# One transpose at a time between single products: a change to the order of TensorE's work in a hybrid encoder layer

## The chip, the cores and the metric

The kernel runs on one core of one Trainium2 chip. The metric is the device time of one execution in microseconds (us). The kernel before took 697.28 us, the median of three runs (695.9 to 697.84).

Names of engines are those of the profile: PE is the matrix engine (TensorE), PEld its loading of stationary operands, DVE, ACT and POOL the vector, scalar and GpSimd engines, SP the engine that issues most transfers. A "product" below is one matmul instruction of a projection.

## The reference

One layer over 512 tokens with 1024 features, in fp32. A pre-norm, one input projection whose columns belong to three groups of attention heads (A: differential, 4 heads; B: forgetting, 6 heads; C: chunked, 6 heads), one output projection into the residual, and then a gated MLP with a causal convolution and a gated per-layer input.

```python
hn = rms_norm(h, ln_mix)
z = hn @ w_in                     # 1024 x 3590
(q1, q2, k1, k2, va, qf, kf, vf, fg, qc, kc, vc) = jnp.split(z, IN_SPLITS, axis=-1)
# every q and k: rms_norm per head of 64
o_a = diff_attention(q1, q2, k1, k2, va, lam, subln_g, lam_init)
log_f = jax.nn.log_sigmoid(fg + fgate_bias)
o_b = forgetting_attention(qf, kf, vf, log_f)     # bias: cumulative sum of log_f
o_c = chunk_attention(qc, kc, vc, rel_bias)
h = h + jnp.concatenate([o_a, o_b, o_c], axis=-1) @ w_out
h = h + conv_gated_mlp(rms_norm(h, ln_ffn), w_up, conv_w, conv_b, w_down)
gate = jax.nn.sigmoid(rms_norm(h, ln_ple) @ w_ple_gate)
h = h + (p @ w_ple_proj) * gate
```

## The kernel before

An fp32 operand is split into a high and a low part, and each fp32 product is made of three products of those parts (`mm3`: high by high, high by low, low by high). The change touches only the first part of the kernel, in which the input projection, the attention and most of the output projection (six of eight blocks of its contraction) share PE.

**Slots.** The work that fills PE comes in slots. Slots 4 to 7 project the part A0b for the four blocks of 128 tokens (262 columns), 8 to 11 A1 (384 columns), 12 to 15 A1b (256), 16 to 27 B0, B1 and B2 and 28 to 39 C0, C1 and C2 (384 each), and slots 40 to 47 are units of the output projection (512 columns, `out_unit`). A projecting slot has eight steps j = 0 to 7 of three products; a slot of the output projection has six steps of three.

**Units between the steps.** The attention of a pair of heads is cut into generators. `qk_cols` brings q and then k into feature-major order: four transposes of 128x128 blocks of `zn` into one bank of PSUM (tile `..._q_p`, then `..._k_p`), then copies by ACT and DVE, then three moves of 64 rows by POOL. `forget_cumsum` transposes the log gates (`pf`), scans along the tokens on DVE (`fs`) and transposes back (`pq`). `scores` makes, for each block of queries, two matmuls into a bank with tag `s` (two buffers), and a softmax on DVE, ACT and POOL, whose result `e` POOL or DVE scales. `prob_cols` transposes the probabilities in three groups (`pt0`: 4 transposes, `pt1`: 3, `ptc`: 3), each followed by a copy on ACT (`pth`) and a subtraction on DVE (`ptl`). `values` multiplies them with V, in two steps of four matmuls. All transposes go into banks with tag `t` (three buffers).

**The order.** The table `T` gives each unit a slot and a step: `"B1a": (24, 1)` is the `qk_cols` of pair B1, from step 1 of slot 24. `run` (line 731) goes through the eight steps of a slot: it takes one step of the filling products, and then one step of the unit at the head of the slot's list, if its time has come. So a group of three or four transposes, with all that follows it up to the unit's next `yield`, stands behind three products. What the list holds after the eighth step is run to its end before the next slot begins, with no product between. PE's instructions are pinned in this order; those of ACT, DVE and POOL in this part are put in order by the framework.

**The rest of the kernel** (MLP, gate) follows with an order of its own by a planner's costs; the change leaves it as it is.

Of the kernel before, what the change touches and what calls it, by code (L numbers as in the profile page):

```python
# [15 lines left out]
P = 128  # L16
D = 1024
S = 512
NT = S // P
KD = D // P  # L20
# [12 lines left out]
C_MIX, C_QK, C_SUB, C_CONV0, C_CONV1, C_CONV2, C_PLE, C_CONVB, C_FFN, C_FGB, C_LAM, NSMALL = (  # L33
    0, 8, 14, 16, 60, 104, 148, 156, 200, 208, 214, 470)
# [43 lines left out]
def kernel(ctx: ExitStack, tc: tile.TileContext, x, xt0, xt, pt_in, small, bias_c,  # L78
# [33 lines left out]
    pe, act, dve, pool, sp = (Engine(e) for e in (nc.tensor, nc.scalar, nc.vector, nc.gpsimd, nc.sync))  # L112
# [30 lines left out]
    def col(c0, i=0):  # L143
        return cols[:, c0 + i : c0 + i + 1]
# [88 lines left out]
    def load_rect(w, k0, nk, c0, ncol, name, eng=dve, gain=None):  # L233
        rows = w[k0 * P : (k0 + nk) * P, c0 : c0 + ncol].rearrange("(k p) c -> p k c", p=P)
        return load_w(lambda raw: [(raw[:, : nk * ncol].rearrange("p (k c) -> p k c", k=nk), rows)],
                      nk, ncol, ncol, name, eng, gain)

    def mm3(acc, ah, al, bh, bl, first, last, **k):
        pe.matmul(acc, ah, bh, start=first, stop=False, **k)
        pe.matmul(acc, ah, bl, start=False, stop=False, **k)  # L240
        pe.matmul(acc, al, bh, start=False, stop=last, **k)
# [11 lines left out]
    def tcol(T, k, t):  # L253
        return T[k // 4][:, k % 4, t * P : (t + 1) * P]
# [164 lines left out]
    def feature_cols(zn, j, name):  # L419
        pt = bank("t", f"{name}_p")  # L420
        for t in range(NT):
            pe.transpose(pt[:, t * P : (t + 1) * P], zn[:, t, j * P : (j + 1) * P], ident)
        return pt

    def move(dst, src):
# [1 line left out]

    def split_q(zn, g, name):

        pt = feature_cols(zn, 0, name)  # L430
        q0, q1 = (ap.tile([P, S], F32R, tag="q", bufs=4, name=f"{name}_q{i}") for i in range(2))
        lo = ap.tile([P, S], F32R, tag="ql", bufs=1, name=f"{name}_ql")
        act.activation(q0, pt, AF.Identity, scale=g)
        dve.scalar_tensor_tensor(lo, pt, g, f32(q0), ALU.mult, ALU.subtract)
        move(q1[DN], q0[DN])
        move(q0[DN], lo[UP])
        move(q1[UP], lo[DN])
        return q0, q1

    def split_k(zn, g, name):  # L440

        pt = feature_cols(zn, 1, name)
# [14 lines left out]
    def project(ws, n, t, z, evac, prefetch):  # L457
        for k in range(KD):
            wh, wl = ws[k // 2]
            mm3(z[:, :n], tcol(Th, k, t), tcol(Tl, k, t), wh[:, k % 2, :], wl[:, k % 2, :], k == 0, k == KD - 1)  # L460
            if k < KD - 1:
                yield
        evac()
        for w in prefetch:
            w()
        yield
# [36 lines left out]
    def qk_cols(pr, part):  # L503
        need(*(("in", pr, part, t) for t in range(NT)))
        g = GAIN[pr[0]]
        zn = ZN[pr, part]
        q = split_q(zn, gq[:, g : g + 1], f"{pr}_q{part}")
        yield
        QK[pr, part] = (q, *split_k(zn, col(C_QK, g + 1), f"{pr}_k{part}"))
        yield  # L510


# [3 lines left out]
    def forget_cumsum():  # L516
        need(*(("in", "A0", 1, t) for t in range(NT)))
        xv = fg[:, :, 0:6]
        fa = ap.tile([P, NT, 6], F32, tag="fa", name="fa")
        dve.scalar_tensor_tensor(fa, xv, -1.0, xv, ALU.mult, ALU.max)  # L520
        act.activation(fa, fa, AF.Exp, scale=-1.0)
        act.activation(fa, fa, AF.Ln, bias=onec)
        dve.scalar_tensor_tensor(xv, xv, 0.0, fa, ALU.min, ALU.subtract)
        yield
        pf = bank("t", "pf")
        for t in range(NT):
            pe.transpose(pf[:, t * P : (t + 1) * P], fg[:, t, :], ident)
        fs = ap.tile([P, S], F32, tag="bias", bufs=3, name="fs")
# [6 lines left out]
        yield  # L535
        pq = bank("t", "pq")
        for t in range(NT):
            pe.transpose(pq[:, t * P : (t + 1) * P], fs[:, t * P : (t + 1) * P], ident)
        dve.tensor_copy(fq[:, :, 0:6], pq.rearrange("p (t c) -> p t c", t=NT)[:, :, 0:6])
        done("fc")  # L540
        yield
# [74 lines left out]
    def prob_cols(pr, hh):  # L616
        probs = PROB[pr, hh]
        tiles = []
        for kb in range(2):
            n = (NT - kb) * P  # L620
            pt = bank("t", f"{pr}_{hh}_pt{kb}")
            for qb in range(kb, NT):
                pe.transpose(pt[:, (qb - kb) * P : (qb - kb + 1) * P], probs[qb][:, kb * P : (kb + 1) * P], ident)
            th = ap.tile([P, S], F32R, tag="pth", bufs=3, name=f"{pr}_{hh}_pth{kb}")
# [4 lines left out]
            yield  # L629
        assert not PTC_OF  # L630
        PTC_OF.append((pr, hh))
        pt = bank("t", f"{pr}_{hh}_ptc")
        pe.transpose(pt[:, P : 2 * P], probs[3][:, 3 * P : 4 * P], ident)
        pe.transpose(pt[:, 2 * P : 3 * P], probs[2][:, 2 * P : 3 * P], ident)
        pe.transpose(pt[:, 3 * P : 4 * P], probs[3][:, 2 * P : 3 * P], ident)
# [67 lines left out]
    def out_unit(j, ks, wts, prefetch):  # L703

        acc = bank("zs"[j % 2] if ks[0] else "z", f"wo_{ks[0]}_{j}")
        c = slice(j % 4 * P, (j % 4 + 1) * P)
        for k in ks:
            wh, wl = (w[:, 0, c] for w in wts[k])
            mm3(acc, wh, wl, Th[k // 4][:, k % 4, :], Tl[k // 4][:, k % 4, :], k == ks[0], k == ks[-1])
# [14 lines left out]
    def step(early, g):  # L724
        if early:
            with tc.high_priority(offset=early):
                next(g)
        else:
            next(g)

    def run(fill, todo):

        todo = [(start, early, gen(*args)) for start, early, gen, args in todo]
        for j in range(8):
            next(fill, None)
            while todo and j >= todo[0][0]:
                try:
                    step(*todo[0][1:])
                    break
                except StopIteration:  # L740
                    todo.pop(0)
# [9 lines left out]
    T = {  # L751
# [139 lines left out]
    for n in range(2):  # L891
        for t in range(NT):
            wts = {k: wo[k, n] for k in range(6)}
            pre = []
            if n == 0:
                pre = [wo_load(k, 1) for k in ((0, 1), (2, 3), (4,), (5,))[t]]
            else:
                pre = [wo_load(6 + t // 2, t % 2)]
            if slot == T["C1v1"][0] + 1:
                split_o(6, 7, slice(0, S))  # L900
            run(out_unit(4 * n + t, range(6), wts, pre), steps.get(slot, []))
            slot += 1
            next_job()
    assert max(COPIES) < slot
# [923 lines left out]
```

## Time and profile before

| | |
|---|---|
| median of three runs | 697.28 us (695.9 to 697.84) |
| profiled execution, first to last instruction (span) | 692.9 us |
| PE busy | 678.8 us, 98% of the span |
| DVE, ACT, POOL busy | 560.7, 411.0, 238.7 us |
| granted TensorE clock | 1.000 |

No time beside its span is given for the profiled execution; the median of the runs is 4.4 us above the span. A row of the timeline or of a group of matmuls gives the start of the first one, the time until the end of the last one, and the number in it. Matmuls are pipelined and their ends are modelled, so costs on PE are read below from start to start. A wait stands in square brackets at the end of a row, with the instruction that ended it. In the tile names the numbers of pairs and heads are left out: `B_pt<-ident,B_e` is a transpose of probabilities of any B pair, `B_z` a projection.

### The profile page before, as it was taken

What the parts mean: (1) busy time and instruction counts of PE and PEld (TensorE: products, weight loads), DVE (VectorE), ACT (ScalarE), POOL (GpSimd) and SP (SyncE); (2) the same over time, 40 slices, a digit from 0 to 9 for tenths busy, and PEclk for the clock granted to TensorE, in tenths of its full rate; (3) what the DMA queues carried; (4) which work ended last, traced back from release to release, by engine and by line L of the source; (5) the groups of instructions that cost most, each with busy time, mean ns of one, the idle gap of its engine ahead of it and who ended that gap; (6) DMA issues with size and microseconds to landing.
All of it is one profiled execution on the core that took longest, in us unless ns stands there. A gap on an engine that the chain in (4) does not pass through costs nothing.

```text
span 692.9 us, 12202 instructions
## 1 busy us (share of the span) xinstructions
PE 678.8 (98%) x4244; PEld 617.7 (89%) x4244; DVE 560.7 (81%) x1168; ACT 411.0 (59%) x799; POOL 238.7 (34%) x349
## 2 busy tenths in 40 slices
PE   9999999999999999999999999999999999999997
PEld 8988989988999988878899899989998898999886
DVE  7678787888778875599788987898888889888863
ACT  7646766757656754475476655456664566556821
POOL 6586766757575540231211212211111210000210
PEclk9999999999999999999999999999999999999999
DMA  9554579746745174379999799998999884463441
GB/s 329 209 155 110 164 229 273 226 155 164 285 137 179 40 270 138 91 181 253 170 263 223 150 254 248 268 227 189 229 308 246 186 226 140 139 232 100 159 122 61
DMA packets 57112, 133.84 MB, mean 193 GB/s; under 512 B 6454, under 2 KB 8118, under 8 KB 57052
## 3 DMA queue, kind: packets, MB, share of 16 engines
q1 hardware_dynamic: 45660, 107.60, 47.3%
q0 software_dynamic: 11104, 25.17, 22.2%
q8 instruction: 33, 0.54, 0.3%
q10 hardware_dynamic: 288, 0.30, 0.1%
q14 instruction: 27, 0.22, 0.1%
HBM read 125.83 MB, written 44.05 MB: 245 GB/s over the span
## 4 chain that ended last, share of the span: by engine, by line
PE 83%; DVE 6%; POOL 3%; DMA 3%; ACT 2%; issue 2%; SPq 0%; POOLq 0%; DVEq 0%; ACTq 0%
PE u L104 22%; PE dn_X L104 9%; PE pg L104 6%; PE wo L104 6%; PE C_z L104 5%; PE sX L104 5%; PE dn_Y L104 4%; PE B_z L104 4%; PE sY L104 3%; PE sZ L104 3%; PE A_z L104 3%; PE dn_Z L104 2%; PE pp L104 2%; PE C_s L104 1%; DMA bias_B<-fk_d 1%
## 5 line engine op out<-in xcount | busy, mean ns | idle before, releaser
L104 DVE TENSOR_TENSOR w_lo<-w_raw,w_hi 128x768 fp32r<-128x768 f32 (+5 forms) x154 | 115.0, 786 | 9.4 <-ACT w_hi L104 9.2
L104 ACT CAST w_hi<-w_raw 128x768 fp32r<-128x768 f32 (+5 forms) x154 | 99.7, 687 | 33.8 <-PE dn_X L104 8.0
L104 PE MATMUL u<-Th,w_hi 128*128 128x512 f32 x224 | 87.0, 391 | 0.0
L104 PE MATMUL u<-Tl,w_hi 128*128 128x512 f32 x224 | 86.9, 390 | 0.0
L104 PE MATMUL u<-Th,w_lo 128*128 128x512 f32 x224 | 86.8, 390 | 0.0
L104 PEld LDWEIGHTS u<-Th,w_lo 128*128 128x128 f32 x224 | 42.0, 188 | 8.9
L104 PEld LDWEIGHTS u<-Th,w_hi 128*128 128x128 f32 x224 | 42.0, 188 | 8.6 <-ACT Th L104 0.4
L104 PEld LDWEIGHTS u<-Tl,w_hi 128*128 128x128 f32 x224 | 42.0, 188 | 8.1
L104 DVE SCALAR_TENSOR_TENSOR c<-u,cols,c 128x511 f32<-128x511 f32 (+1 forms) x56 | 41.0, 745 | 6.2 <-ACT c L104 5.7
L104 POOL DMA_DIRECT2D usum<-usum x16 | 13.0, 813 | 91.2 <-DMA usum<-in_w_up_dram 49.3
L104 PE MATMUL dn_X<-g_ah,w_hi 128*128 128x256 f32 x144 | 39.8, 276 | 0.0
L104 PE MATMUL dn_X<-g_ah,w_lo 128*128 128x256 f32 x144 | 39.8, 276 | 0.0
L104 PE MATMUL dn_X<-g_al,w_hi 128*128 128x256 f32 x144 | 39.8, 276 | 0.0
L104 PE MATMUL B_z<-B_h,Th 128*128 128x384 f32 x96 | 34.4, 358 | 0.7 <-DVE B_zn L104 0.6
L104 PE MATMUL C_z<-C_h,Th 128*128 128x384 f32 x96 | 34.3, 357 | 0.0
L104 PE MATMUL B_z<-B_h,Tl 128*128 128x384 f32 x96 | 32.3, 337 | 0.0
L104 PE MATMUL C_z<-C_h,Tl 128*128 128x384 f32 x96 | 32.3, 337 | 0.0
L104 PE MATMUL C_z<-C_l,Th 128*128 128x384 f32 x96 | 32.2, 336 | 0.0
L104 PE MATMUL B_z<-B_l,Th 128*128 128x384 f32 x96 | 32.2, 335 | 0.0
L104 POOL DMA_DIRECT2D dsum<-dsum x16 | 13.0, 814 | 53.5 <-DMA dsum<-dsum 24.5
L104 POOL TENSOR_TENSOR sums<-sums,n_sq 128x512 f32<-128x512 f32 x3 | 3.9, 1297 | 79.7 <-ACT n_sq L104 79.6
L104 ACT ACTIVATE c<-u,cols 128x512 f32<-128x512 f32 x28 | 21.5, 775 | 16.0 <-PE u L104 14.6
(504 smaller groups left out, 2385.4 us busy)
## 6 DMA issues: line engine op xcount, KB each, us to landing
w_raw<-in_w_up_dram SPq DMA_DIRECT2D x44, 384.0 KB, 6.9
dsum<-in_w_dsum_dram SPq DMA_DIRECT2D x12, 768.0 KB, 8.1
w_raw<-dsum SPq DMA_DIRECT2D x24, 384.0 KB, 5.9
usum<-in_w_usum_dram SPq DMA_DIRECT2D x32, 256.0 KB, 6.1
w_raw<-in_w_down_dram SPq DMA_DIRECT2D x18, 384.0 KB, 5.3
w_raw<-usum SPq DMA_DIRECT2D x16, 384.0 KB, 7.4
B_r<-in_w_in_dram SPq DMA_DIRECT2D x12, 384.0 KB, 3.7
C_r<-in_w_in_dram SPq DMA_DIRECT2D x12, 384.0 KB, 5.9
```

What stands on the lines that cost most here:

```text
L104: ins = getattr(self.eng, op)(*a, **k)
```

## The change

- `project` and `out_unit` yield after every product, not after every three (`mm3_singly`; a value `ONE` says that a group of three isn't finished).
- Every generator with transposes yields `ONE` after each transpose but the last of a group. The last one is emitted together with the copies that follow it, as before.
- Before the first transpose of a group stands a yield `NEXT_COLS`, or the unit starts in that state (`FIRST_AT`).
- `run` puts at most one transpose behind each product. A group in progress goes on behind every product; a new one begins behind the second product of a step, or behind the third, where all other units go on as before.
- What the list holds at the end of a slot is run on until a unit stands at a transpose (`ONE` or `NEXT_COLS`); it and all behind it are carried into the next slot, ahead of its own list, with step 0. Only the last slot runs all to the end.

The table `T`, the number of instructions and their operands stay as they are.

```diff
+    ONE, NEXT_COLS = "one", "cols"
+
+    def mm3_singly(acc, ah, al, bh, bl, first, last):
+        for i, (a, b) in enumerate(((ah, bh), (ah, bl), (al, bh))):
+            pe.matmul(acc, a, b, start=first and i == 0, stop=last and i == 2)
+            if i < 2:
+                yield ONE
...
         for t in range(NT):
             pe.transpose(pt[:, t * P : (t + 1) * P], zn[:, t, j * P : (j + 1) * P], ident)
+            if t < NT - 1:
+                yield ONE
         return pt
...
-            mm3(z[:, :n], tcol(Th, k, t), tcol(Tl, k, t), wh[:, k % 2, :], wl[:, k % 2, :], k == 0, k == KD - 1)
+            yield from mm3_singly(z[:, :n], tcol(Th, k, t), tcol(Tl, k, t), wh[:, k % 2, :], wl[:, k % 2, :], k == 0, k == KD - 1)
...
-        q = split_q(zn, gq[:, g : g + 1], f"{pr}_q{part}")
-        yield
-        QK[pr, part] = (q, *split_k(zn, col(C_QK, g + 1), f"{pr}_k{part}"))
+        q = yield from split_q(zn, gq[:, g : g + 1], f"{pr}_q{part}")
+        yield NEXT_COLS
+        k = yield from split_k(zn, col(C_QK, g + 1), f"{pr}_k{part}")
+        QK[pr, part] = (q, *k)
         yield
...
             for qb in range(kb, NT):
                 pe.transpose(pt[:, (qb - kb) * P : (qb - kb + 1) * P], probs[qb][:, kb * P : (kb + 1) * P], ident)
+                if qb < NT - 1:
+                    yield ONE
...
-        else:
-            next(g)
-
-    def run(fill, todo):
-
-        todo = [(start, early, gen(*args)) for start, early, gen, args in todo]
+                return next(g)
+        return next(g)
+
+    FIRST_AT = {qk_cols: NEXT_COLS, prob_cols: NEXT_COLS}
+    LEAD = 2
+
+    class Unit:
+
+        def __init__(self, start, early, gen, args):
+            self.start, self.early, self.g, self.at = start, early, gen(*args), FIRST_AT.get(gen)
+
+        def go(self):
+            try:
+                self.at = step(self.early, self.g)
+            except StopIteration:
+                self.at = "end"
+            return self.at
+
+    CARRY = []
+
+    def run(fill, todo, last=False):
+
+        todo = CARRY + [Unit(*q) for q in todo]
+        CARRY.clear()
         for j in range(8):
-            next(fill, None)
-            while todo and j >= todo[0][0]:
-                try:
-                    step(*todo[0][1:])
+            busy = False
+            for i in range(3):
+                more = next(fill, None)
+                if todo and (todo[0].at == ONE or todo[0].at == NEXT_COLS and j >= todo[0].start and not busy and i >= 3 - LEAD and more == ONE):
+                    busy = todo[0].at != ONE or busy
+                    todo[0].go()
+                if more != ONE:
                     break
-                except StopIteration:
-                    todo.pop(0)
+            while not busy and todo and todo[0].at != ONE and j >= todo[0].start:
+                if todo[0].go() != "end":
+                    break
+                todo.pop(0)
         for _ in fill:
             pass
-        for _, early, g in todo:
-            try:
-                while True:
-                    step(early, g)
-            except StopIteration:
-                pass
+        for i, q in enumerate(todo):
+            while q.at != "end":
+                if q.at in (ONE, NEXT_COLS) and not last:
+                    CARRY.extend(todo[i:])
+                    for q in CARRY:
+                        q.start = 0
+                    return
+                q.go()
```

More of the change, by code (lines that the diff above doesn't have):

```diff
@@ L428, in split_q @@
     def split_q(zn, g, name):
-        pt = feature_cols(zn, 0, name)
+        pt = yield from feature_cols(zn, 0, name)
         q0, q1 = (ap.tile([P, S], F32R, tag="q", bufs=4, name=f"{name}_q{i}") for i in range(2))
@@ L440, in split_k @@
     def split_k(zn, g, name):
-        pt = feature_cols(zn, 1, name)
+        pt = yield from feature_cols(zn, 1, name)
         k0, k1 = (ap.tile([P, S], F32R, tag="k", bufs=4, name=f"{name}_k{i}") for i in range(2))
@@ L523, in forget_cumsum @@
         dve.scalar_tensor_tensor(xv, xv, 0.0, fa, ALU.min, ALU.subtract)
-        yield
+        yield NEXT_COLS
         pf = bank("t", "pf")
@@ L527, in forget_cumsum @@
             pe.transpose(pf[:, t * P : (t + 1) * P], fg[:, t, :], ident)
+            if t < NT - 1:
+                yield ONE
         fs = ap.tile([P, S], F32, tag="bias", bufs=3, name="fs")
@@ L534, in forget_cumsum @@
         nc.sync.dma_start(out=fk_d, in_=nf)
-        yield
+        yield NEXT_COLS
         pq = bank("t", "pq")
@@ L538, in forget_cumsum @@
             pe.transpose(pq[:, t * P : (t + 1) * P], fs[:, t * P : (t + 1) * P], ident)
+            if t < NT - 1:
+                yield ONE
         dve.tensor_copy(fq[:, :, 0:6], pq.rearrange("p (t c) -> p t c", t=NT)[:, :, 0:6])
@@ L623, in prob_cols @@
                 pe.transpose(pt[:, (qb - kb) * P : (qb - kb + 1) * P], probs[qb][:, kb * P : (kb + 1) * P], ident)
+                if qb < NT - 1:
+                    yield ONE
             th = ap.tile([P, S], F32R, tag="pth", bufs=3, name=f"{pr}_{hh}_pth{kb}")
@@ L628, in prob_cols @@
             tiles.append((th[:, :n], tl[:, :n]))
-            yield
+            yield NEXT_COLS
         assert not PTC_OF
@@ L632, in prob_cols @@
         pt = bank("t", f"{pr}_{hh}_ptc")
-        pe.transpose(pt[:, P : 2 * P], probs[3][:, 3 * P : 4 * P], ident)
-        pe.transpose(pt[:, 2 * P : 3 * P], probs[2][:, 2 * P : 3 * P], ident)
-        pe.transpose(pt[:, 3 * P : 4 * P], probs[3][:, 2 * P : 3 * P], ident)
+        for c, qb, kb in ((1, 3, 3), (2, 2, 2), (3, 3, 2)):
+            pe.transpose(pt[:, c * P : (c + 1) * P], probs[qb][:, kb * P : (kb + 1) * P], ident)
+            if c < 3:
+                yield ONE
         th, tl = ptc
@@ L708, in out_unit @@
             wh, wl = (w[:, 0, c] for w in wts[k])
-            mm3(acc, wh, wl, Th[k // 4][:, k % 4, :], Tl[k // 4][:, k % 4, :], k == ks[0], k == ks[-1])
+            yield from mm3_singly(acc, wh, wl, Th[k // 4][:, k % 4, :], Tl[k // 4][:, k % 4, :], k == ks[0], k == ks[-1])
             if k != ks[-1]:
@@ L726, in step @@
             with tc.high_priority(offset=early):
-                next(g)
-        else:
-            next(g)
-    def run(fill, todo):
-        todo = [(start, early, gen(*args)) for start, early, gen, args in todo]
-        for j in range(8):
-            next(fill, None)
-            while todo and j >= todo[0][0]:
-                try:
-                    step(*todo[0][1:])
+                return next(g)
[15 more added lines that the diff above has]
+        CARRY.clear()
+        for j in range(8):
+            busy = False
[5 more added lines that the diff above has]
+                if more != ONE:
                     break
-                except StopIteration:
-                    todo.pop(0)
+            while not busy and todo and todo[0].at != ONE and j >= todo[0].start:
+                if todo[0].go() != "end":
+                    break
+                todo.pop(0)
         for _ in fill:
             pass
-        for _, early, g in todo:
-            try:
-                while True:
-                    step(early, g)
-            except StopIteration:
-                pass
+        for i, q in enumerate(todo):
[6 more added lines that the diff above has]
+                q.go()
     T = {
@@ L900 @@
                 split_o(6, 7, slice(0, S))
-            run(out_unit(4 * n + t, range(6), wts, pre), steps.get(slot, []))
+            run(out_unit(4 * n + t, range(6), wts, pre), steps.get(slot, []), n == 1 and t == NT - 1)
             slot += 1
```

## The prediction, made before the changed kernel was run

> **What bounds the kernel now.** I read the page first, then busy time by stretches, then PE's timeline around each wait in the part that changes.
>
> ```profile
> span 692.9 us, 12202 instructions
> ...
> PE 678.8 (98%) x4244; PEld 617.7 (89%) x4244; DVE 560.7 (81%) x1168; ACT 411.0 (59%) x799; POOL 238.7 (34%) x349
> ```
> ```profile
> 28.00:262.00 234.00, 225.32 (x1382) 208.85 (x1382) 188.76 (x575) 154.02 (x370) 150.57 (x223) 1.00 0.58 178
> 262.00:272.00 10.00, 10.00 (x52) 8.37 (x52) 7.53 (x14) 6.18 (x12) 0.21 (x1) 1.00 0.59 187
> 272.00:693.00 421.00, 416.47 (x2649) 375.19 (x2648) 346.25 (x541) 231.71 (x382) 69.81 (x82) 1.00 0.76 193
> ```
>
> PE is the bound: 98% busy at the full clock (1.00 behind the counts in the rows by stretches). The change acts from about 28 us (slot 6) to a little behind 262 us. Up to 262 us PE is idle for 234.00 - 225.32 = 8.7 us, behind it for 4.5 in 431; read from start to start the waits cost more, since a matmul that waited also has to load its operand afterwards. The change adds no instruction. It can win through the price of a transpose on PE, or through waits; it loses through prices and waits too. I take these in turn.
>
> **The price of a transpose.** Slot 40, with no wait in it:
>
> ```profile
> 243.87 0.60 PE L104 MATMUL C_pt<-ident,C_e 128*128 128x128 f32 x4
> 244.22 0.48 PE L104 MATMUL wo<-Th,wo_h 128*128 128x512 f32 x1
> 244.54 0.39 PE L104 MATMUL wo<-Tl,wo_h 128*128 128x512 f32 x1
> 244.77 0.39 PE L104 MATMUL wo<-Th,wo_l 128*128 128x512 f32 x1
> 245.00 0.49 PE L104 MATMUL C_pt<-ident,C_e 128*128 128x128 f32 x3
> 245.24 0.48 PE L104 MATMUL wo<-Th,wo_h 128*128 128x512 f32 x1
> 245.56 0.39 PE L104 MATMUL wo<-Tl,wo_h 128*128 128x512 f32 x1
> ```
>
> A product of 512 columns takes 244.77 - 244.54 = 0.23. From the first of four transposes to the second product behind them it is 0.67, so four cost 0.67 - 0.23 = 0.44; three cost 245.56 - 245.00 - 0.23 = 0.33. That is 0.11 each, with nothing left over for the change from transposes to products, within the rounding of the rows. The product behind a group starts early on paper (244.22) and takes 0.32 to the next one: it still sits out the last transpose. So the last transpose of a group, which already has a product behind it, costs as much as one with another transpose behind it, and I expect a single one to cost 0.11. By the diff and the loops there are 248 transposes, and the places where one is followed by something else go from 59 (one for each uninterrupted run) to 236. For the 177 new ones I take 0.005 us each, between 0 and the 0.01 that the rows can hide: **+0.9** (0 to +1.8). Less than nothing would need the cheaper transpose that is the first rival.
>
> By the Trainium skill, page "TensorE: Matmul & The Clock Gate", section "LDWEIGHTS (loading the stationary operand)", loading 128 columns takes 128/1.2 = 107 ns (an estimate from its formula). The spacing of 0.11 agrees with that; by that rule the product behind a single transpose has its own 107 ns of load uncovered, which speaks against any gain from singles.
>
> **Waits that should go.** Slot 20 ends with four scores of A1 run back to back:
>
> ```profile
> 109.67 0.28 PE L104 MATMUL A_0b_s<-A_k_k,A_q_q 128*128 128x256 f32 x1
> 109.79 0.28 PE L104 MATMUL A_0b_s<-kl,A_q_q 128*128 128x256 f32 x1
> 110.38 0.38 PE L104 MATMUL A_s<-A_k_k,A_q_q 128*128 128x256 f32 x1 [0.31 <-DVE A_st L104]
> 110.59 0.28 PE L104 MATMUL A_s<-kl,A_q_q 128*128 128x256 f32 x1
> 110.92 0.38 PE L104 MATMUL A_1b_s<-A_k_k,A_q_q 128*128 128x256 f32 x1
> ```
>
> A matmul of 256 columns takes 0.12. So 0.59 - 0.12 = 0.47 is lost for the bank, 0.21 - 0.12 = 0.09 for the late load, 0.33 - 0.12 = 0.21 for the next bank, and 0.1 for its load: 0.87. Now `prob_cols` of A1 is in mid-group at the end of slot 20 and is carried, with these scores behind it; they then stand between the steps of slot 21. I take **-0.8** (-0.9 to -0.5).
>
> Slots 24 and 25:
>
> ```profile
> 141.47 0.33 PE L104 MATMUL B_z<-B_h,Tl 128*128 128x384 f32 x1
> 141.64 0.40 PE L104 MATMUL B_po<-B_pth,B_V 128*128 128x512 f32 x1
> 142.30 0.50 PE L104 MATMUL B_po<-B_ptl,B_V 128*128 128x512 f32 x1 [0.26 <-DVE B_ptl L104]
> ...
> 144.38 0.34 PE L104 MATMUL B_z<-B_h,Tl 128*128 128x384 f32 x1
> 145.27 0.38 PE L104 MATMUL B_s<-B_k_k,B_q_q 128*128 128x256 f32 x1 [0.55 <-POOL B_k_k L104]
> ...
> 147.96 0.47 PE L104 MATMUL B_s<-B_k_k,B_q_q 128*128 128x512 f32 x1 [0.55 <-DVE B_st L104]
> ```
> ```profile
> 143.20 0.64 POOL L561 TENSOR_SCALAR_AFFINE_SELECT dg<-bias_B 128x512 f32<-128x512 f32 x1 [1.18 <-DMA bias_B<-fk_d]
> ```
>
> A product of 384 columns takes 0.17 (141.47 to 141.64). B1's q and k are now transposed in a heap at the end of slot 24. POOL's last move of k stands behind the mask `dg`, which waits for the transfer of its bias until 143.20, and the first scores of B1 wait 145.27 - 144.38 - 0.17 = 0.72, and 0.1 for the load. After the change B1's transposes are carried into the first three steps of slot 25, and all of its scores slide to that slot's end, well behind the moves: **-0.8** (-0.9 to 0). The price is that they stand there in a heap of four, where now only the last one does, with 0.55 idle. The nearest heap of four is that of slot 20, 0.87, with smaller blocks; DVE reads a B bank in two instructions, so I take 1.3 for the heap against the 0.7 (idle and load) now: **+0.6** (+0.2 to +0.9). The values of B0 lose 142.30 - 141.64 - 0.23 = 0.43 and the load for `ptl`, behind the DVE work of the heap of slot 24. That work is spread then, but the gap before them shrinks (below): **-0.3** (-0.5 to +0.5).
>
> The transposes of q that wait for their fourth block of `zn`:
>
> ```profile
> 166.93 0.49 PE L104 MATMUL B_q_p<-ident,B_zn 128*128 128x128 f32 x3
> 167.84 0.33 PE L104 MATMUL B_q_p<-ident,B_zn 128*128 128x128 f32 x1 [0.42 <-DVE B_zn L104]
> ```
> ```profile
> PE C_q_p L104 <- DVE C_zn L104: 0.7, 1, 0.7
> ```
>
> B2 loses 167.84 - 166.93 - 3 x 0.11 = 0.58, and C0, by 0.7 idle, more. In both, three products now stand between the first transpose and the fourth: 3 x 0.17 = 0.5 of work in the wait, **-1.0** for both (-1.2 to -0.5). A0b waits in the same way, but there the gain is given back:
>
> ```profile
> 43.91 0.33 PE L104 MATMUL A_q_p<-ident,A0b_zn 128*128 128x128 f32 x1 [0.66 <-DVE A0b_zn L104]
> ```
> ```profile
> 47.45 2.00 POOL L104 TENSOR_SCALAR A_k_k<-A_k_k 64x512 fp32r<-64x512 f32 x3
> ```
> ```profile
> 49.51 0.39 PE L104 MATMUL A_0b_s<-A_k_k,A_q_q 128*128 128x256 f32 x1
> ```
>
> `zn` sets 43.91; from there POOL's moves, in their order, run until 47.45 + 2.00 = 49.45, and the first scores with A0b start at 49.51. Whatever PE wins at 43.91 it waits at 49.51: **0**.
>
> **Waits that should grow.** A group now ends two to five products later against its neighbours, its copies start later, and whoever reads them stands where it stood. The scan of the forget gates:
>
> ```profile
> 59.93 0.66 PE L104 MATMUL pq<-ident,fs 128*128 128x128 f32 x4 [0.93 <-DVE fs L104]
> ```
> ```profile
> 58.66 1.21 DVE L104 TENSOR_TENSOR_SCAN fs<-f_ones,pf 128x512 f32<-128x512 f32 x1
> ```
>
> `pf` ends two products later (0.35), and `pq` still starts behind the last product of slot 11: **+0.3** (0 to +1.0, if DVE puts one of its 0.9 us splits ahead of the scan). Values that follow their transposes in the same slot, as for B1:
>
> ```profile
> 173.22 0.39 PE L104 MATMUL B_po<-B_ptl,B_V 128*128 128x512 f32 x1
> ```
> ```profile
> 172.26 1.15 DVE L104 TENSOR_TENSOR B_ptl<-B_pt,B_pth 128x512 fp32r<-128x512 f32 x2
> ```
>
> The first of these two subtractions, about 0.65 of the 1.15, ends near 172.9: 0.3 to spare, and the gap shrinks by two products, 0.35. So a wait of 0.05 and a load: **+0.2** (0 to +0.5); A0, with narrower products (0.12): **+0.1** (0 to +0.3). Scores behind the moves of k: A1b **+0.1** (0 to +0.5), and C2, where the transposes of q and k run over into slot 41:
>
> ```profile
> 251.74 0.39 PE L104 MATMUL wo<-Th,wo_l 128*128 128x512 f32 x1
> 252.55 0.39 PE L104 MATMUL C_s<-C_k_k,C_q_q 128*128 128x256 f32 x1 [0.41 <-POOL C_k_k L104]
> ```
> ```profile
> 251.88 0.61 POOL L104 TENSOR_SCALAR C_k_k<-C_k_k 64x512 fp32r<-64x512 f32 x1
> ```
>
> Here q ends one product later (0.23) and k five (1.15). POOL's last move ends at 252.49, after an unbroken row of six that q starts, so I take **+0.2** (0 to +1.1). The transposes of A1's q may find their bank still being read: **+0.1** (0 to +0.3).
>
> Sum: +0.9 - 0.8 - 0.8 + 0.6 - 0.3 - 1.0 + 0.3 + 0.2 + 0.1 + 0.1 + 0.2 + 0.1 = **-0.4 us**. Behind 262 us PE hardly ever waits, so a shift passes to the end: span 692.5. The profiled execution's span lies 4.4 us under the median of the runs, 697.28; so I forecast **696.9 us**, which is no change: 0.3%, about what a measurement of this kernel can tell from none, is 2.1 us. Adding the lower ends gives -3.3, the upper ones +5.9.
>
> **The rivals.**
>
> *The load is hidden.* If 0.11 is a load that a product in front can cover, only the transpose's own streaming is left. 512 columns take 0.23 and 256 take 0.12, so 128 stream in 0.055; 248 x 0.055 = 13.6 us less, 683.6. Against it stands that the first transpose of a group has a product in front and the group still costs 0.11 for each. The same page of the Trainium skill, in "Part 2: What happens when you issue a matmul", has PE pull loads ahead of running matmuls; by that rule a single transpose would be covered. The early start on paper of the product at 244.22 would fit it, the 0.32 behind it doesn't.
>
> *Waits go, and none comes.* Copies have slack, and PE gains 0.9 + 0.9 + 1.2 + 0.5, less 0.4 for the heap: -3.1, or 694.2. For it: DVE and ACT get their work in smaller lots. Against it: three of the slacks above are under 0.35.
>
> *The copies come late* (slower). The place: `pq`, the values of A0, B0 and B1, the scores of A1b and C2. It decides where the slack is under the delay of 0.35 (five products at C2). Priced at 1.0 for `pq`, 0.45 (0.35 and a load) for each of three values, 1.3 for the scores, 0.3 for the bank and 1.8 for the change-overs, 5.8, less the 2.0 that slots 20, 25, 28 and 32 still win net: +3.8, or 701.1. For it: A0b's k move and C2's end within 0.06 of the scores that need them. Against it: most groups feed values a slot later.
>
> **Numbers.** No change (696.9, alone 695.2 to 699.4): 0.41. Hidden load: 0.07. Waits go: 0.27. Copies late: 0.25. So faster 0.34, same 0.41, slower 0.25; the range from 693.0 to 701.5 takes in the other two rivals, leaves out the hidden load, and is a little narrower than all ends added, which won't fall together. The order that the framework gives DVE, ACT and POOL may move by more than these terms; that is why it isn't narrower.
>
> **What would show it.** A single transpose: from its start to the second product behind it one product and 0.11 (0.055 for the first rival). The waits for `A_st` near 110 and `B_k_k` near 145 are gone, and four scores of B1 stand in a row near 147 with two waits. The waits for `B_zn` near 168 and for `C_zn` are 0.5 shorter, that for `fs` near 60 is 0.3 longer. I am wrong if a transpose's price moves, or if DVE or POOL takes its work in another order, so that waits show at tiles that I don't name.

## The result, and the profile after

The changed kernel took **704.21 us** (median of four runs, 702.91 to 704.73); the kernel before, beside it, took 697.21. The ratio is **1.0107, 95% interval 1.0088 to 1.0125**: slower by 7.0 us, where no change was forecast. The time lies outside the range of 693.0 to 701.5.

The head of the page after:

```profile
span 703.0 us, 12202 instructions
```

The two spans differ by 703.0 - 692.9 = 10.1 us, the medians by 7.0. The profiled execution after took 704.73, so 1.73 us lie outside its span. With as much outside the span of 692.9, the profiled execution before took about 694.6, 2.6 under its median. So rows of the two traces explain 10.1 us, of which some 3 are the difference between one execution and another. Two of the kernels below have one execution far longer than its others (2406.23 and 964.85 us), which is left out of their times and ratios.

Busy time by stretches, after (columns: the stretch, its length, busy time and count of PE, PEld, DVE, ACT and POOL, then granted clock, DMA share and GB/s):

```profile
28.00:272.00 244.00, 230.35 (x1392) 211.71 (x1391) 191.66 (x577) 154.57 (x371) 148.97 (x224) 0.99 0.55 170
272.00:703.00 431.00, 426.25 (x2700) 383.20 (x2698) 353.40 (x553) 237.28 (x394) 69.64 (x82) 1.00 0.75 193
```

The part behind the change still takes 431.00 us. All 10.0 us lie in the stretch ahead of it: 244.00 for 234.00. Of these, 0.87 came earlier still: slot 4's first product starts at 22.53, where it was 21.66, before any transpose has moved, and in the traces of the other kernels below it starts between 21.42 and 22.50, whatever their order; I take this for a difference of executions. PE is idle in the stretch for 13.65 us where it was 8.68, which is 5.0 more; and the clock is 0.99 where it was 1.00, which costs 3.4 (below). That leaves 0.7 us, which is not traced further. What PE waited for in that stretch, after and then before (idle us in total, times, longest):

```profile
PE B_s L104 <- DVE B_st L104: 3.2, 4, 1.8
PE pq L104 <- DVE fs L104: 3.1, 1, 3.1
PE B_z L104 <- ACT B_sq L104: 1.5, 1, 1.5
...
PE C_s L104 <- POOL C_k_k L104: 0.8, 1, 0.8
...
PE B_ptc L104 <- DVE kl L104: 0.7, 1, 0.7
```
```profile
PE B_s L104 <- DVE B_st L104: 0.9, 2, 0.5
```

Three waits carry the loss: the scan of the forget gates (`fs`), the scores of B1 (`B_st`), and a projection that waits for `B_sq`, at a place where nothing waited before. (A shorter wait of the same kind, 0.62 for `B_zn` at 104.09 before, is gone.)

**The scan.** DVE before, on both sides of the scan, which started at 58.66:

```profile
57.79 0.96 DVE L104 TENSOR_TENSOR B_l<-B_r,B_h 128x768 fp32r<-128x768 f32 x1
...
59.79 0.93 DVE L104 TENSOR_TENSOR B_l<-B_r,B_h 128x768 fp32r<-128x768 f32 x1
60.64 1.10 DVE L104 SCALAR_TENSOR_TENSOR A_e<-A_e,A_st,A_3b_e 128x512 f32<-128x512 f32 x1
```

PE after, then DVE, then POOL:

```profile
59.98 0.42 PE L104 MATMUL A_z<-A_h,Tl 128*128 128x384 f32 x1
63.52 0.47 PE L104 MATMUL pq<-ident,fs 128*128 128x128 f32 x1 [3.13 <-DVE fs L104]
```
```profile
59.16 1.83 DVE L104 TENSOR_TENSOR B_l<-B_r,B_h 128x768 fp32r<-128x768 f32 x2
61.58 0.75 DVE L104 SCALAR_TENSOR_TENSOR A_e<-A_e,A_st,A_3b_e 128x512 f32<-128x512 f32 x1 [0.59 <-POOL A_3b_e L104]
62.25 1.21 DVE L104 TENSOR_TENSOR_SCAN fs<-f_ones,pf 128x512 f32<-128x512 f32 x1
```
```profile
59.19 2.36 POOL L104 TENSOR_SCALAR A_3b_e<-A_3b_e,A_3b_st,nlam 128x512 f32<-128x512 f32 x1 [1.70 <-DVE A_3b_st L104]
```

The reader is to follow DVE's queue (a split is an instruction that makes the low part `B_l` of a weight). Before, the scan stood between two splits, ahead of `A_e`; now it stands behind both splits and behind `A_e`, which itself waits for POOL until 61.55. The last `pf` starts at 59.95, but the scan only at 62.25. From start to start PE loses 63.52 - 59.98 = 3.54, less 0.17 for the product and 0.09 for the rest of a single transpose: 3.3, where it was 1.1.

**The clock.** Stretches of the trace after, same columns as above:

```profile
58.00:63.50 5.50, 2.39 (x16) 2.06 (x14) 4.84 (x8) 3.68 (x7) 3.24 (x2) 1.00 0.60 156
63.50:67.00 3.50, 3.48 (x17) 3.48 (x17) 1.46 (x4) 0.38 (x1) 2.45 (x6) 0.51 0.83 208
...
151.00:155.50 4.50, 1.84 (x10) 1.14 (x9) 2.54 (x13) 1.34 (x4) 3.08 (x5) 1.00 0.06 21
155.50:159.20 3.70, 3.70 (x16) 3.09 (x15) 2.11 (x14) 1.94 (x6) 1.44 (x3) 0.54 0.20 65
```

In this execution PE's clock fell to half in just two places of this part: behind the wait for the scan, and behind the waits for `B_st`. Each took about 3.4 us, so each costs 1.7 us of work (3.5 x 0.49 and 3.7 x 0.46). By the row of 58.00, PE had been busy for 2.39 of 5.50 us before the first; by that of 151.00, for 1.84 of 4.50 before the second. The Trainium skill, page "TensorE: Matmul & The Clock Gate", section "Why this matters for your kernels", asks for no idle gap of PE over some 3 us; the first place (3.13 idle) agrees, the second has no gap as long as that, and no single wait over 1.8.

**The scores of B1.** PE, POOL and DVE after:

```profile
151.45 0.39 PE L104 MATMUL B_s<-B_k_k,B_q_q 128*128 128x256 f32 x1 [0.20 <-POOL B_k_k L104]
...
153.97 0.44 PE L104 MATMUL B_s<-B_k_k,B_q_q 128*128 128x384 f32 x1 [1.78 <-DVE B_st L104]
154.25 0.34 PE L104 MATMUL B_s<-kl,B_q_q 128*128 128x384 f32 x1
155.27 0.47 PE L104 MATMUL B_s<-B_k_k,B_q_q 128*128 128x512 f32 x1 [0.68 <-DVE B_st L104]
```
```profile
148.69 0.64 POOL L576 TENSOR_SCALAR_AFFINE_SELECT dg<-bias_B 128x512 f32<-128x512 f32 x1 [1.31 <-DMA bias_B<-fk_d]
149.41 1.99 POOL L104 TENSOR_SCALAR B_k_k<-B_k_k 64x512 fp32r<-64x512 f32 x3
151.50 0.30 POOL L104 TENSOR_SCALAR B_rs<-B_rs,rstd 128x4 f32<-128x4 f32 x1
151.88 1.04 POOL L104 TENSOR_TENSOR B_rs<-B_rs,nhalf 128x4 f32<-128x4 f32 x1
```
```profile
152.96 0.42 DVE L104 SCALAR_TENSOR_TENSOR B_zn<-B_z,B_rs 128x256 f32<-128x256 f32 x1 [2.12 <-POOL B_rs L104]
```

The heap of four scores is where the prediction put it. Its price is not: DVE's reads of the scores stand in its queue behind `B_zn`, which waits for `B_rs` on POOL, and that stands behind three moves of k, and these behind the mask `dg`, which waits for its transfer. So the late mask still ends in a wait of PE, by way of a norm that has nothing to do with the scores. This chain is read from the trace; no run below changes POOL's or DVE's order there by itself.

**The projection of slot 21.** PE, then ACT, then DVE after:

```profile
113.81 0.27 PE L104 MATMUL A_ptc<-ident,A_e 128*128 128x128 f32 x1
115.63 0.42 PE L104 MATMUL B_z<-B_h,Th 128*128 128x384 f32 x1 [1.55 <-ACT B_sq L104]
```
```profile
113.83 0.48 ACT L104 CAST A_pth<-A_pt 128x384 fp32r<-128x384 f32 x1 [0.29 <-PE A_pt L104]
114.20 0.37 ACT L104 ACTIVATE B_V<-B_z,rstd 128x128 fp32r<-128x128 f32 x1
115.19 0.38 ACT L104 ACTIVATE B_sq<-B_z 128x256 f32<-128x256 f32 x1 [0.61 <-DVE B_V L104]
```
```profile
113.57 1.32 DVE L104 TENSOR_TENSOR A_ptl<-A_pt,A_pth 128x512 fp32r<-128x512 f32 x2 [0.93 <-ACT A_pth L104]
114.81 0.34 DVE L104 SCALAR_TENSOR_TENSOR B_V<-B_z,rstd,B_V 128x128 fp32r<-128x128 f32 x1
```

The four scores that waited at the end of slot 20 stand between products now, and their waits are gone, as forecast. But the groups of transposes in front of them end later, their copies `A_pth` and `A_ptl` come later, and ACT and DVE do those before they empty the projection's bank. Slot 21's first product waits for that bank.

### The profile page after: what moved, and what is told of

It is laid out like the page before. It is cut to its first block, busy times and chain, and to the rows that moved or that the text cites. A ratio compares the mean times of both kernels' runs of the same rounds, so it can differ in the third digit from the quotient of the medians.

```text
span 703.0 us, 12202 instructions
## 1 busy us (share of the span) xinstructions
PE 683.2 (97%) x4244; PEld 619.8 (88%) x4244; DVE 562.3 (80%) x1168; ACT 410.6 (58%) x799; POOL 233.8 (33%) x349
## 4 chain that ended last, share of the span: by engine, by line
PE 85%; DVE 7%; POOL 4%; ACT 2%; issue 2%; DMA 1%; SPq 0%; POOLq 0%; DVEq 0%; ACTq 0%
PE u L104 22%; PE dn_X L104 9%; PE C_z L104 6%; PE pg L104 6%; PE wo L104 6%; PE B_z L104 5%; PE sX L104 5%; PE dn_Y L104 4%; PE sY L104 3%; PE sZ L104 3%; PE A_z L104 2%; PE dn_Z L104 2%; PE A1b_z L104 1%; PE C_s L104 1%; PE C_po L104 1%
## 5 line engine op out<-in xcount | busy, mean ns | idle before, releaser
L104 PE MATMUL B_z<-B_h,Tl 128*128 128x384 f32 x96 | 35.6, 371 | 0.0
L104 PE MATMUL C_z<-C_h,Tl 128*128 128x384 f32 x96 | 34.8, 363 | 0.0
L104 PE MATMUL B_z<-B_l,Th 128*128 128x384 f32 x96 | 34.8, 362 | 0.0
L104 PE MATMUL C_z<-C_l,Th 128*128 128x384 f32 x96 | 34.4, 358 | 0.0
```

What stands on the lines that cost most here:

```text
L104: ins = getattr(self.eng, op)(*a, **k)
```

## The experiments

The theory: going singly and carrying cost PE next to nothing; they move the copies behind the transposes, ACT, DVE and POOL get another order, and waits come at three places, two of them with the half clock behind. Rival A: a single transpose is dearer than the rows show, everywhere. Rival B: carrying is what costs, wherever it happens. All ratios are to the kernel before, run on the same chip (695.99 to 696.35 us there); they are taken over all runs, so they aren't exactly quotients of the medians in the column of times.

| kernel | time, us | ratio | interval |
|---|---|---|---|
| carry only | 696.48 | 1.0004 | 0.9987 to 1.0021 |
| singles only | 700.05 | 1.0055 | 1.0037 to 1.0072 |
| changed, `pq` later | 700.41 | 1.0059 | 1.0040 to 1.0077 |
| changed, `pq`'s wait filled | 702.75 | 1.0095 | 1.0076 to 1.0114 |
| changed, `pf` whole | 700.14 | 1.0061 | 1.0045 to 1.0076 |
| before, `pq` later | 696.38 | 1.0003 | 0.9987 to 1.0019 |
| singles only, `pq` later | 696.27 | 0.9997 | 0.9983 to 1.0011 |
| changed, `pq` later, no carry at slot 24 | 697.85 | 1.0022 | 1.0011 to 1.0032 |
| singles, `pq` later, carry at slot 24 only | 698.22 | 1.0027 | 1.0013 to 1.0042 |
| changed, `pq` and B1's scores later | 702.25 | 1.0092 | 1.0060 to 1.0124 |
| carry only, `pq` and B1's scores later | 703.04 | 1.0102 | 1.0076 to 1.0127 |
| singles only, `pq`, C2 and B1's second later | 699.61 | 1.0047 | 1.0031 to 1.0064 |

### The two halves of the change

*Carry only* leaves the groups whole (no `yield ONE`, products by threes) and keeps the carrying:

```diff
-                yield ONE
```

> Transposes stay in whole groups behind three products, as before the change; only the carrying of leftovers into the next slot is kept. Theory (the loss is waits made by the new order, and two drops of the clock behind the two longest): pq follows pf as before, its wait is about 1.1 us and no drop near 60; B1's scores still stand in a heap at the end of slot 25 (waits of about 2 to 3 us, perhaps a drop behind them); 699 to 701. Rival A (a transpose alone costs more on PE): 697, as there are no singles. Rival B (the carrying is what costs): 704.

No change, under what the theory gave, and about where rival A put it. B1's scores do wait in its profiled execution (1.9 us idle for `B_st`), with half the clock behind them, but other waits go in return: B1's for its k, and the 0.7 for `C_zn` before C0's q, are not in its list. Rival B falls: carrying whole groups costs nothing net, to within some 1.5 us.

*Singles only* runs what a slot leaves over to its end, as before:

```diff
-                if q.at in (ONE, NEXT_COLS) and not last:
+                if False:
```

> Single transposes as in the change, but each slot runs its leftovers out at its end, as before. Theory: the wait for pq of 3.3 us and the drop of the clock behind it stay (about 3.7 more than before), the heap of B1's scores is gone, 0.8 for change-overs: 700 to 702. Rival A: 704 or more. Rival B: 697.

As the theory had it: 3.9 us slower, with the wait for the scan at 3.1 idle. Rival A at its full price (704 or more) doesn't fit; at a smaller one it is still open here.

### The scan

*Changed, `pq` later* makes `pq` a unit of its own, at step 7 of slot 12:

```diff
-        yield NEXT_COLS
+        FS.append(fs)
+        yield
...
+    def forget_cols():
+        fs = FS[0]
...
-        "A0a": (6, 6), "A0b": (9, 4), "fc": (11, 5), "A1a": (16, 2)
+        "A0a": (6, 6), "A0b": (9, 4), "fc": (11, 5), "fq": (12, 7), "A1a": (16, 2)
```

> The changed kernel, with the four transposes of pq taken out of slot 11 and put behind the values of slot 12, some 20 products later; nothing else. Theory: the wait of 3.3 us goes, and with it the drop of the clock near 64 (0.5 for 3.4 us, 1.5 lost): 4 to 5 us less than the changed kernel, 699 to 700.5, mean clock 0.997. Rivals A and B: at most the 1.1 that the wait costs before the change, 703.

(1.0107 - 1.0059) x 697 = 3.3 us less, uncertain by some 1.8 us, since both ratios are: inside the forecast time, a little under the 4 to 5. *Before, `pq` later* is the same edit in the kernel before:

> The kernel before with only pq moved to step 7 of slot 12, groups whole and nothing carried. Theory: the wait for the scan (1.09 us from start to start) goes and nothing takes its place: 1.1 us under the kernel before, ratio 0.997 to 0.9995. Rival (another wait takes its place, or the chain to the scores of B sets): the same time as before, ratio 1.000.

The rival held: no gain. The wait went, and another came, in the waits of its profile:

```profile
PE A_pt L104 <- DVE A_e L104: 1.0, 1, 1.0
```

So before the change the wait of 1.1 us at this place cost nothing net, since it covered one behind it; by this reading, only what goes beyond 1.1 is a loss.

*`pq`'s wait filled* puts 24 bf16 products of 256 columns, whose results are not used, ahead of `pq`, so that PE isn't idle for long:

```diff
+        for _ in range(24):
+            pe.matmul(pq[:, 0 : 2 * P], wt.broadcast_to([P, P]), wt.broadcast_to([P, 2 * P]), start=True, stop=True)
```

> The changed kernel with 24 dummy bf16 matmuls of 256 columns on PE, about 0.11 us each, ahead of the first transpose of pq, into the bank that pq then overwrites: the wait is filled and stays as long. Theory: the clock does not drop near 64, so about 1.5 us less than the changed kernel, 702.5, mean clock 0.997. If the drop is not due to the idle PE: no less, 704 to 705.

The clock kept up behind the scan, but the half clock behind B1's scores lasted twice as long in this execution:

```profile
62.20:66.00 3.80, 3.61 (x31) 3.61 (x32) 1.63 (x6) 1.06 (x3) 3.00 (x7) 1.00 0.76 186
```
```profile
152.00:158.80 6.80, 6.16 (x22) 5.29 (x22) 3.91 (x21) 3.58 (x10) 2.74 (x5) 0.50 0.15 39
```

The scan is as late as in the changed kernel, products stand in the wait, and there is no drop. That fits idle time of PE as what makes the drop, but it is one execution of each kernel, and a drop doesn't always follow: singles only has the same wait of 3.1 us in its trace, and one of its four executions has a mean clock of 1.000 (by estimate, half the clock for 3.4 of 699 us makes 0.998). The times differ by only (1.0107 - 1.0095) x 697 = 0.8 us, within the intervals, so the 1.7 us of a drop are read from the trace, not from the time.

*`pf` whole* undoes one yield of the change: `pf`'s four transposes go back to back again, all others singly.

```diff
         for t in range(NT):
             pe.transpose(pf[:, t * P : (t + 1) * P], fg[:, t, :], ident)
-            if t < NT - 1:
-                yield ONE
```

> The changed kernel with one group whole: the four transposes of pf are issued back to back again, so that pf ends two products (0.35 us) earlier; pq and all else stay single and carried. Theory (by that delay of 0.35 us the framework's order for DVE puts a split of 0.9 us and the combination A_e, which itself waits for POOL, ahead of the scan): the scan stands ahead of both again and starts near 59 us, the wait before pq is 1.1 to 1.5 us from start to start for 3.3, no half clock follows it, and the time falls by 2.2 + 1.6 = 3.8 to 700.4 (699.5 to 701.5), ratio 1.005 to 1.007. Rival (the scan is late because pf or its own inputs are late, whatever DVE's order): the wait shrinks by 0.35 at most, the half clock stays, 703.5 to 704.5, ratio over 1.009.

700.14: the one yield is worth as much as moving `pq`. DVE and PE of this kernel:

```profile
58.61 0.96 DVE L104 TENSOR_TENSOR B_l<-B_r,B_h 128x768 fp32r<-128x768 f32 x1
59.49 1.21 DVE L104 TENSOR_TENSOR_SCAN fs<-f_ones,pf 128x512 f32<-128x512 f32 x1
60.62 0.93 DVE L104 TENSOR_TENSOR B_l<-B_r,B_h 128x768 fp32r<-128x768 f32 x1
61.47 1.10 DVE L104 SCALAR_TENSOR_TENSOR A_e<-A_e,A_st,A_3b_e 128x512 f32<-128x512 f32 x1
```
```profile
60.76 0.33 PE L104 MATMUL pq<-ident,fs 128*128 128x128 f32 x1 [1.10 <-DVE fs L104]
```

The scan stands between the two splits again, and the idle time ahead of `pq` is back at 1.10 (0.93 before the change, 3.13 after). The whole group still begins behind the second product of its step, as in the changed kernel, so `pf` ends three products earlier here than there (0.52 us), not two as the expectation has it, and one product earlier than before the change. So a delay of half a microsecond or less in one group of transposes turned DVE's order over, and with it came the 2.2 us of longer wait. Whether the framework goes by times or by the order in which the instructions are written, no run tells: the edit moves both.

### Singles, without carrying and without that wait

*Singles only, `pq` later* joins the edits of the second and third kernel.

> Single transposes, nothing carried, pq at step 7 of slot 12. Compared with the kernel before with pq moved in the same way, the difference is the price of going singly. Theory: 0.005 us for each of some 177 change-overs, 0.9, and about 1 us of waits in B1: 1 to 2.5 us above that kernel, 696 to 698. Rival A (singles dearer by 0.02 each): 4 to 5 above it, 699 to 700. Rival B (carrying): the same as the kernel before with pq moved, within 0.5.

Its time is that of the kernel before with `pq` moved (0.9997 against 1.0003), under what the theory gave. Rival A needed 4 to 5 us here and falls: transposing singly costs nothing net, to within some 1.5 us. Rival B named this time, but carry only has already shown that carrying alone is free as well. What costs is the two together: single transposes that are carried. The price of one can be read in the kernel as changed, in slot 20 (seven transposes, with one product of 384 columns between each two):

```profile
111.78 0.27 PE L104 MATMUL A_pt<-ident,A_e 128*128 128x128 f32 x1
...
113.52 0.27 PE L104 MATMUL A_pt<-ident,A_e 128*128 128x128 f32 x1
```

Six periods take 1.74, so 0.29 each, less 0.175 for the product: 0.115, where a transpose in a group takes 0.11.

### Which carry

With `pq` moved and all transposes single, everything carried is 1.0059 and nothing carried 0.9997: 4.3 us. Two kernels divide them.

```diff
-                if q.at in (ONE, NEXT_COLS) and not last:
+                if q.at in (ONE, NEXT_COLS) and not last and slot != 24:
```

> The changed kernel with pq moved to step 7 of slot 12, and in slot 24 alone nothing is carried: B1's transposes are run to their end there, as in the kernel before. With everything carried the ratio was 1.0059 (700.4 us), with nothing carried 0.9997 (696.3). Theory (the second half of the loss is the carrying of single transposes at this one place: B1's k is late, four scores stand in a heap, and the half clock follows): the loss goes, 696.0 to 697.3, ratio 0.9995 to 1.002; the waits for B_st near 150 us are at most 0.8 from start to start and no drop of the clock follows them. Rival (the loss is spread over the carries of slots 20 and 26 and the rest): 699 to 700.5, ratio over 1.004.

> The complement: singles, pq at step 7 of slot 12, and only what slot 24 leaves over is carried. Theory (slot 24's carry is the second half of the loss): 699.5 to 701, ratio 1.004 to 1.007, with waits for B_st of 1.5 to 2 and about 0.8 behind slot 25 and in most runs a drop of the clock. Rival (spread over the carries): 696 to 697.5, ratio under 1.002.

The second has `slot == 24` in that place. Both come out half-way, and neither the theory (slot 24 alone) nor its rival holds. Slot 24's carry costs (1.0027 - 0.9997) x 696 = 2.1 us, or by the other pair (1.0059 - 1.0022) x 696 = 2.6; the rest 1.7 to 2.2; each of these is uncertain by some 1.5 us. The first kernel's profile shows waits that belong to the rest:

```profile
PE B_z L104 <- ACT B_sq L104: 1.5, 1, 1.5
```

The wait of slot 21 stays, and C2's with 0.8 too. In the second kernel the first isn't in the list and C2's is 0.4, but B1's scores wait:

```profile
148.09 0.44 PE L104 MATMUL B_s<-B_k_k,B_q_q 128*128 128x384 f32 x1 [1.05 <-DVE B_st L104]
```

The next score waits 0.68. The ten runs of this kernel spread with their granted clock: four with 0.999 or 1.000 took 696.15 to 697.28 us, the six with 0.996 to 0.998 took 698.01 to 700.11. Whether the clock drops varies from run to run. The four have a mean of 696.74 us, which is 0.7 above the 696.07 of the kernel before at the same clocks on this chip (14 of its 23 runs), and the six have 699.10: so most of what slot 24's carry costs is the clock, as far as runs can be sorted by it afterwards. The first kernel has 0.999 or 1.000 in all its ten runs, so a drop of the clock has no part in its loss.

### Attempts to move the waits away

*B1's scores later*, in the changed kernel and in carry only, both with `pq` moved:

```diff
-"B1s0": (25, 4), "B1s1": (26, 0), "B1p0": (26, 7)
+"B1s0": (26, 3), "B1s1": (27, 0), "B1p0": (27, 5)
```

> The changed kernel with pq moved to step 7 of slot 12, and the scores of B1 moved from (25, 4) and (26, 0) to (26, 3) and (27, 0), pt0 of B1 to (27, 5). Theory (the loss is waits made by the changed order on DVE, ACT and POOL, plus the half clock that follows them): with only pq moved the ratio was 1.0059, about 700.4 us against 696.1; the heap of B1 scores lost 2.8 us to waits and 1.7 to the half clock. Both should go, little of it come back: 696.5 (695.5 to 698.0), ratio 0.999 to 1.003, no drop of the clock between 140 and 165 us, and the waits for B_st in slot 25 and 26 under 0.7 each. Rival A (a transpose by itself is dearer than its start-to-start cost shows, some 0.02 us for each of the 248): the time stays above 700. Rival B (carrying work into the next slot is what costs): above 699, since everything is carried still.

> Groups whole, leftovers carried, pq at step 7 of slot 12 and B1's scores at (26, 3) and (27, 0), pt0 of B1 at (27, 5). Theory: carrying alone was 1.0004, with 1.09 us of wait at pq, about 1.9 in B1's scores and 1.7 of half clock behind them; without these 693 to 695, ratio 0.995 to 0.998, under the kernel before. Rival B (carrying costs by itself): 696 to 697, ratio 1.000.

Both are slower by 6 to 10 us than forecast. The trace of the second shows one of the new waits, and half the clock behind it; for the first there is no trace of an ordinary execution, so its waits stay open.

```profile
PE B_q_p L104 <- DVE B_zn L104: 4.1, 1, 4.1
```
```profile
174.00:180.00 6.00, 5.83 (x22) 5.60 (x23) 4.78 (x9) 2.91 (x5) 4.30 (x8) 0.51 0.91 293
```

There `B_zn` waits for `B_rs` on POOL, and this norm stands behind a scaling of probabilities, `B_e` (0.98 us from 170.85), by its place one of B1's later scores.

*Two steps*: singles only, `pq` later, C2's scores at (41, 4) and B1's second probabilities at (29, 1).

> Singles, nothing carried, pq at step 7 of slot 12, and two units one step later: C2's first scores (41, 4) for (41, 3), B1's second probabilities (29, 1) for (29, 0). In the version without these two the waits were 0.57 us before C2's scores and 0.85 before the last group of B1's probabilities, from start to start, and the time that of the kernel before, 696.3. Theory (each of these waits is a local slack that a step covers): 1.0 to 1.4 us less, 694.9 to 695.3, ratio 0.998 to 0.9985. Rival (the order of DVE and POOL moves with each step, and a wait comes elsewhere, as in the two runs in which B1's scores were moved): 696 to 699, ratio 1.000 or more.

The rival held: 3.5 us more than without the two steps (1.0047 against 0.9997), with waits elsewhere that the version without them doesn't list.

```profile
PE C_z L104 <- DVE C_zn L104: 1.8, 1, 1.8
PE C_q_p L104 <- DVE B_ptl L104: 1.4, 1, 1.4
```

No version beat the kernel before; the best are level with it.

## Why the prediction was wrong, point by point

- **Price of a transpose** (+0.9 for 177 change-overs at 0.005): right by the rows, 0.115 against 0.11. Net of the waits that singles win, nothing was left of it in the time.
- **The scan** (+0.3, 0 to +1.0): **this is the step that failed first.** The upper end named the right event, a split ahead of the scan, but not that `A_e` would come with it and wait for POOL. It measured +2.2 from start to start, and 3.2 to 3.3 with what follows, by the two kernels that undo it.
- **The heap of B1's scores** (+0.6, 0.2 to 0.9) **and B1's k** (-0.8): this is the second step that failed, right in place and wrong in size. Idle for `B_st` rose from 0.9 to 3.2, and that for the moves fell from 0.55 to 0.20, so the pair measured about +1.9 of idle for a forecast of -0.2. The heap of slot 20 was the wrong model: there DVE was free to read the scores, here it stood behind a norm that waited for POOL. By the pair of kernels for slot 24, carrying there costs 2.1 to 2.6.
- **The heap of A1's scores** (-0.8): these waits went, but a wait of 1.55 for the projection's bank came in their place. The prediction asked who waits for the late copies among the readers of the copies, not among what stands behind the copies on ACT and DVE.
- **Waits of q** (-1.0), **values of B0** (-0.3), **A0b** (0): right, but for A0b in size; the waits for `B_zn` and `C_zn` before q and for `B_ptl` are gone from the list, and those of A0b's q stay (1.46 idle for 1.29, with 0.19 more ahead of its scores).
- **C2** (+0.2, 0 to +1.1): 0.79 idle where it was 0.41, so +0.4, within the bounds. **Values of A0 and B1** (+0.1, +0.2): no such wait shows. `B_ptc`, with 0.7, was named nowhere; "waits show at tiles that I don't name" was so for it and for `B_z`.
- **The clock**: no term at all. The prediction priced a wait at its own length. Both drops of the profiled execution stand behind waits that came or grew with the change, 1.7 us each.
- **The rival "copies come late"** gave 701.1 and the sign; it is the nearest to what happened, but it priced delays at their own length, 0.35, while a delay that changes an order costs as much as what gets in front. That its sign came true is in part luck: 1.35 of its 5.8 us stood at values (A0, B0, B1) at which no wait shows, and 1.8 at change-overs that cost nothing net; without them its 3.8 would have been 0.65.
- **Forecast from the span**: of the 4.4 us between span and median some 1.75 lie outside the span, and 2.6 are this execution's place among the runs. The forecast, of the median, isn't moved by it.

How the loss divides, by differences of ratios: the scan 3.2 to 4.0 us, the carries of single transposes 3.6 to 4.3 (slot 24 about half; the rest by the waits at slot 21 and C2, which no run takes away alone), single transposes 0 by themselves. Open is how much of the scan's part is clock: only one run fills a wait, and its time couldn't tell.

## What to carry to other kernels

Where only one engine's order is written out and a framework orders the others, a move of half a microsecond or less can turn over the order of a queue, and then costs what gets in front, not the delay: look at each in-order queue at the place, with what its neighbours wait for, before pricing a delay. Ask of a late copy not only who reads it but what stands behind it on its engine. And where PE has been thinly busy for some microseconds, allow for a drop of the clock on top of the price of the wait.

## What was not expected of the hardware

**A wait of PE can cost more than itself.** The drops to half clock lasted 3.4 or 6.8 us and came behind 3.1 us of idle time, and also where PE was busy 1.84 of 4.50 us with no wait over 1.8; in carry only one came behind a stretch in which PE was busy 3.04 of 4.60 us, with no wait over 1.3. They don't come each time. In the kernel with `pf` whole the same heap, with waits of 1.6 and 0.8 from start to start, had no drop in its profiled execution:

```profile
148.00:160.00 12.00, 9.47 (x56) 8.26 (x55) 9.83 (x51) 6.36 (x20) 5.26 (x10) 1.00 0.10 27
```

**POOL slows down beside DVE's splits.** The same operation, 128x512 on POOL, three times: before, beside one split; after, beside two (59.19, above, 2.36 us); and after, in A1's second pass:

```profile
57.82 1.57 POOL L104 TENSOR_SCALAR A_3b_e<-A_3b_e,A_3b_st,nlam 128x512 f32<-128x512 f32 x1 [1.70 <-DVE A_3b_st L104]
```
```profile
125.12 0.77 POOL L104 TENSOR_SCALAR A_3b_e<-A_3b_e,A_3b_st,nlam 128x512 f32<-128x512 f32 x1
```

0.77, 1.57 and 2.36: about 0.8 more for each split of 0.95 beside it, as if POOL stood still for most of it. Other traces repeat it: 1.57 and 1.58 beside one split (carry only, `pf` whole), 2.35 or 2.36 beside two (singles only, and the changed kernel with `pq` later or filled). The splits put ahead of the scan so cost twice: their own time on DVE, and that of `A_3b_e`, which `A_e` and then the scan wait for. The Trainium skill, page "GPSIMD Engine Reference", section "Specifications", says that its SBUF interfaces are shared with the vector engine and contend with instructions of two SBUF inputs; these rows agree and give the size.
